# New constants in the duration model that sets the order of emission

## Chip, cores and metric

The kernel runs on one core of a Trainium2 chip. The metric is the device time of one execution in microseconds (us). Engines are called by name: TensorE (PE; PEld is its loading of weights), VectorE (DVE), ScalarE (ACT), GpSimd (POOL) and SyncE (SP), which issues nearly all transfers.

## What is computed

One step of a decoder trunk in float32, for one prompt of 256 tokens and 8 samples of 8 tokens, 320 tokens together. The width is 2048. Cut to its frame, the reference is:

```python
def trunk(x, c, states, p):
    for li in range(2):
        h, gate = modulate(x, c, ada_w, ada_b, norm_g)   # rmsnorm(x) * (1 + scale) + shift; silu(c) @ ada_w + ada_b
        if li == 0:
            z = h @ ab_w_in                              # q, k, v, r, g_lr, u
            o, s_gla = gla_mix(q, k, v, log_a, s0)       # gated linear attention, 4 heads
            y, h_re, h_im = s5_mix(u, ...)               # complex diagonal scan
            out = concat([o, y * sigmoid(y @ w_glu + b)]) @ ab_w_out
        else:
            z = h @ ml_w_in                              # q, k, v, og, gates
            hh, c1, n1, m1 = mlstm_mix(q, k, v, i_pre, logf, c0, n0, m0)   # 4 heads, a 512 x 256 state each
            out = (head_rmsnorm(hh) * sigmoid(og)) @ ml_w_out
        x = x + gate * out
        h, gate = modulate(x, c, ffn_ada_w, ffn_ada_b, ffn_norm_g)
        x = x + gate * ((silu(h @ w1) * (h @ w3)) @ w2)
    return rmsnorm(x), new states
```

## The kernel before

Activations stand feature-major, 128 features by 320 tokens. Every large product streams its weights through TensorE as 128 x 128 blocks. A float32 product is three passes of a shorter float format: weights and activations are split into a high and a low part, and each block gives three products of 320 columns (`hi` with `xh`, `lo` with `xh`, `hi` with `xl`). These are called stream products here; there are 18336. `load_to` loads a unit of 512 KB (24 stream products) from four buffers ahead, and `split_to` makes `hi` on ScalarE and `lo` on VectorE.

Everything else runs between the blocks as tasks, which are Python generators: the GLA and S5 mixers of layer 0, the mLSTM of layer 1, and the adaLN products (`Ada`: 192 steps, each with 1 MB of weights in one of two buffers and four products of 512 columns). After every three stream products `tick` looks at the tasks. It resumes one when the model says that what the task waits for is there (`due` asks `est.ready`), and when VectorE and ScalarE are not too far ahead of TensorE in the model.

The model is the class `Est`. Each instruction that is emitted is noted in it: `note` starts it when its engine and its operands are free, adds a duration from a formula, and keeps when the result can be read. A transfer gets an issue time, a time of the descriptor generator (`DGE`), bytes at a fixed rate on one server (`DMA`) and 1.0 us to land. No duration of the model is in the program that runs: it sets only which instruction is emitted before which. Where the program must wait for a task, `idle` and `wait` take adaLN steps or emit a product that nobody reads (`warm`), until the model's time has passed.

In the mLSTM (`ml_task`) each of 32 steps takes one sample's state, 512 KB, from one of three buffers `CR`: `load_c(g + 2)` at the end of step g, `store(g - 1)` at its beginning, both on SP's queue. `Ada.drip` takes one adaLN step every `gap` ticks at most, if `spare` finds its weights there in the model; `gap` is 2 in the first FFN.

## Time and profile before

| | us |
|---|---|
| median of 3 runs | 3397.55 |
| lowest and highest run | 3381.38 and 3400.94 |
| span of the profiled execution, first to last instruction | 3383.8 |
| TensorE busy in it | 3287.9 |
| VectorE busy in it | 1870.4 |
| ScalarE busy in it | 1327.8 |

For the profiled execution the span is the time that is known; it lies 13.8 us below the median of the runs and within their spread. Busy times of TensorE are modelled at their ends, so the starts of its instructions are the firmer number.

### The profile page before, as it was taken

The page shows a single profiled execution, that of the slowest core. Times are in us where ns is not written, and L with a number is a line of the kernel's source. Part 1 is how long each engine was busy: PE and PEld are TensorE (multiplying, and loading weights), DVE is VectorE, ACT ScalarE, POOL GpSimd, SP SyncE. Part 2 cuts the span into 40 slices and gives each one's busy share as a digit, 9 for nine tenths or more (in the row PEclk, how much of TensorE's full clock was granted, in tenths as well). Part 3 has the DMA queues.
Part 4 walks back from the last instruction along what each step waited for, and adds up shares of the span by engine and source line. Part 5 has one row for each costly group of instructions (what it writes and reads, how often), then busy time and mean ns, then how long its engine had stood idle before and what let it go on. Part 6 is the DMA issues. An engine that isn't in the chain of part 4 may idle for free.

```text
span 3383.8 us, 57931 instructions
## 1 busy us (share of the span) xinstructions
PE 3287.9 (97%) x22802; PEld 3023.7 (89%) x22802; DVE 1870.4 (55%) x3921; ACT 1327.8 (39%) x2509; POOL 336.9 (10%) x508
## 2 busy tenths in 40 slices
PE   7899889999999999999999999999999999999998
PEld 4687778887877799999998899999899999999997
DVE  3768767663344345445465665566645545545546
ACT  2354554343323333433434433344433343343343
POOL 0225511220000000000031000002200000000002
PEclk9999999999999999999999999999999999999999
DMA  9886678779999954444455665556564444444443
GB/s 305 291 264 219 194 259 305 269 240 322 317 318 320 320 171 149 150 152 148 151 170 145 191 194 144 177 187 206 184 207 149 152 150 150 150 150 150 150 150 100
DMA packets 597794, 686.66 MB, mean 203 GB/s; under 512 B 41097, under 2 KB 495057, under 8 KB 596945
## 3 DMA queue, kind: packets, MB, share of 16 engines
q1 hardware_dynamic: 594464, 680.26, 61.7%
q8 instruction: 179, 2.93, 0.3%
q10 hardware_dynamic: 3056, 2.70, 0.2%
q14 instruction: 95, 0.77, 0.1%
HBM read 643.19 MB, written 39.69 MB: 202 GB/s over the span
## 4 chain that ended last, share of the span: by engine, by line
PE 87%; DMA 5%; DVE 4%; ACT 2%; POOL 1%; issue 1%; SPq 0%; ACTq 0%; DVEq 0%; POOLq 0%
PE mm L220 74%; PE misc L220 8%; PE ada L220 5%; DVE S_slab L220 1%; POOL S_slab L220 1%; DVE lo L220 1%; DMA fix_slab<-in_ffn_ada_w_dram 1%; DVE X_slab L220 1%; DVE G_slab L220 1%; DMA R_slab<-in_state_mlstm_C_dram 1%; DMA fix_slab<-in_ab_w_in_dram 0%; DMA fix_slab<-in_ml_ada_w_dram 0%; DMA G_slab<-in_ab_ada_w_dram 0%; DMA fix_slab<-in_ab_ada_w_dram 0%; ACT hi L220 0%
## 5 line engine op out<-in xcount | busy, mean ns | idle before, releaser
L220 DVE TENSOR_TENSOR lo<-fix_slab,hi 128x512 fp32r<-128x512 f32 (+1 forms) x1556 | 1087.1, 704 | 1173.0 <-ACT hi L220 1168.9
L220 ACT CAST hi<-fix_slab 128x512 fp32r<-128x512 f32 (+1 forms) x1556 | 944.3, 612 | 1425.2 <-PE mm L220 1366.6
L220 PE MATMUL mm<-xh,hi 128*128 128x320 f32 x4704 | 1491.6, 317 | 9.7 <-DVE S_slab L220 5.9
L220 PE MATMUL mm<-xl,hi 128*128 128x320 f32 x4704 | 1460.7, 311 | 0.8 <-DVE xl L220 0.6
L220 PE MATMUL mm<-xh,lo 128*128 128x320 f32 x4704 | 1460.1, 310 | 0.9 <-DVE lo L220 0.9
L220 PEld LDWEIGHTS mm<-xh,hi 128*128 128x128 f32 x4704 | 888.4, 189 | 121.8 <-issue 88.0
L220 PEld LDWEIGHTS mm<-xh,lo 128*128 128x128 f32 x4704 | 889.2, 189 | 2.4 <-DVE lo L220 1.8
L220 PEld LDWEIGHTS mm<-xl,hi 128*128 128x128 f32 x4704 | 888.1, 189 | 2.2 <-DVE xl L220 2.2
L220 PE MATMUL mm<-ffh,hi 128*128 128x320 f32 x1408 | 437.8, 311 | 0.0
L220 PE MATMUL mm<-ffh,lo 128*128 128x320 f32 x1408 | 434.3, 308 | 0.0
L220 PE MATMUL mm<-ffl,hi 128*128 128x320 f32 x1408 | 434.3, 308 | 0.0
L220 POOL TENSOR_TENSOR X_slab<-X_slab 128x320 f32<-128x320 f32 (+1 forms) x117 | 109.9, 940 | 2062.4 <-DVE X_slab L220 2016.1
L220 PEld LDWEIGHTS mm<-ffh,hi 128*128 128x128 f32 x1408 | 264.4, 188 | 18.4 <-issue 17.6
L220 PEld LDWEIGHTS mm<-ffh,lo 128*128 128x128 f32 x1408 | 264.5, 188 | 0.0
L220 PEld LDWEIGHTS mm<-ffl,hi 128*128 128x128 f32 x1408 | 264.3, 188 | 0.0
L220 PE MATMUL ada<-fix_slab 128*32 128x512 f32 x1432 | 193.9, 616 | 12.7 <-DMA fix_slab<-in_ab_ada_w_dram 8.7
L220 POOL TENSOR_TENSOR S_slab<-S_slab 128x32 f32<-128x32 f32 (+3 forms) x226 | 119.5, 538 | 78.3 <-ACT S_slab L220 34.1
L220 DVE SCALAR_TENSOR_TENSOR ffs<-ffs,mm 128x320 f32<-128x320 f32 x176 | 81.4, 488 | 29.9 <-ACT ffs L220 23.8
L220 DVE SCALAR_TENSOR_TENSOR X_slab<-mm,fix_slab,X_slab 128x256 f32<-128x256 f32 x176 | 84.6, 480 | 16.7 <-PE mm L220 16.5
L220 PE MATMUL misc<-fix_slab 128*128 128x128 f32 (+1 forms) x454 | 73.1, 287 | 5.7 <-ACT fix_slab L220 5.6
L220 PEld LDWEIGHTS misc<-fix_slab 128*128 128x128 f32 x454 | 59.2, 171 | 18.2 <-ACT fix_slab L220 7.0
L220 PEld LDWEIGHTS ada<-fix_slab 128*32 128x32 f32 x1432 | 29.0, 108 | 51.0 <-issue 34.0
(151 smaller groups left out, 1812.9 us busy)
## 6 DMA issues: line engine op xcount, KB each, us to landing
fix_slab<-in_ffn_w_dram SPq DMA_DIRECT2D x524, 512.0 KB, 3.5
fix_slab<-in_ffn_ada_w_dram SPq DMA_DIRECT2D x96, 1024.0 KB, 7.6
fix_slab<-in_ml_ada_w_dram SPq DMA_DIRECT2D x48, 1024.0 KB, 7.2
fix_slab<-in_ml_w_in_dram SPq DMA_DIRECT2D x96, 512.0 KB, 4.4
fix_slab<-in_ab_ada_w_dram SPq DMA_DIRECT2D x35, 1024.0 KB, 8.0
fix_slab<-in_ab_w_in_dram SPq DMA_DIRECT2D x64, 512.0 KB, 6.5
R_slab<-in_state_mlstm_C_dram SPq DMA_DIRECT2D x32, 512.0 KB, 4.1
out_dram<-R_slab SPq DMA_DIRECT2D x32, 512.0 KB, 6.5
```

The source lines that it names most:

```text
L220: r = call(*a, **k)
```

## The change

Only the model's numbers are changed. Stream products get 0.0105 us more each, 0.1468 us instead of 0.1363. Plain float32 products get 0.04 us less where they are wide. A change between kinds of product (stream, products of 32 rows, others) costs TensorE 0.22 or 0.1 us more. The transfer server runs at 395 GB/s instead of 360, and SP's and ScalarE's transfers have a descriptor generator each. VectorE, ScalarE, GpSimd, the issue time and the landing time keep their formulas.

```diff
     def __init__(self):
-        self.t = dict.fromkeys(("PE", "DVE", "ACT", "POOL", "SP", "DGE", "DMA"), 0.0)
+        self.t = dict.fromkeys(("PE", "DVE", "ACT", "POOL", "SP", "DGESP", "DGEACT", "DMA"), 0.0)
         self.wr, self.rd, self.alias = {}, {}, {}
         self.end = 0.0
+        self.kind = None
...
                 self.t[eng] = t + 0.06
-                t = self.t["DGE"] = max(self.t["DGE"], t) + 0.45
-            t = self.t["DMA"] = max(self.t["DMA"], t + 0.65) + 4e-3 * int(np.prod(out.shape)) / 360
+                t = self.t["DGE" + eng] = max(self.t["DGE" + eng], t) + 0.45
+            t = self.t["DMA"] = max(self.t["DMA"], t + 0.65) + 4e-3 * int(np.prod(out.shape)) / 395
             fin = t + 1.0
...
                 elif ins[0].dtype == F32R:
-                    d = n / 2400 + 0.003
+                    d = n / 2400 + 0.0135
                 else:
-                    d = max(1.67e-3 * n + 0.05, 0.2 + 5e-4 * n)
+                    d = max(1.67e-3 * n + 0.01, 0.22)
+
+                kind = "stream" if ins[0].dtype == F32R and n == T else "tiles" if ins[0].shape[1] == 32 else "other"
+                if kind != self.kind:
+                    d += 0.22 if self.kind is None or "stream" in (kind, self.kind) else 0.1
+                self.kind = kind
```

The instructions are the same on every engine, but for 8 `warm` products (327 products of their form before, 319 now) and two elementwise operations that VectorE now does in place of GpSimd. On TensorE the kinds of product change 900 times in the old order and 877 times in the new. What moves is where the tasks stand in the stream.

First place: TensorE in `ml_task`, from the state update (`km`, `vs`) of the fifth step of the first head. `mm` rows are stream products, and the `misc` rows from `fix_slab` are the first of the next step. Before:

```order
L220 MATMUL misc1_17083<-km_16132,vs_16131 128x256 x2
L220 MATMUL misc2_17087<-km_16132,vs_16131 128x256 x2
L220 MATMUL mm_16954<-xh_95,hi0_83 128x320
L220 MATMUL mm_16954<-xh_95,lo0_89 128x320
L220 MATMUL mm_16954<-xl_96,hi0_83 128x320
L220 MATMUL mm_16955<-xh_95,hi0_83 128x320
L220 MATMUL mm_16955<-xh_95,lo0_89 128x320
L220 MATMUL mm_16955<-xl_96,hi0_83 128x320
```

Now:

```order
L226 MATMUL misc0_16987<-km_16104,vs_16103 128x256 x2
L226 MATMUL misc1_16991<-km_16104,vs_16103 128x256 x2
L226 MATMUL mm_16640<-xh_95,hi1_84 128x320
L226 MATMUL mm_16640<-xh_95,lo1_90 128x320
L226 MATMUL mm_16640<-xl_96,hi1_84 128x320
L226 MATMUL misc2_16999<-fix_slab_80 128x128
L226 MATMUL misc0_17003<-fix_slab_80,R_slab_16099 128x128 x4
L226 MATMUL misc1_17009<-fix_slab_80,R_slab_16099 128x128 x4
```

Between this update and the next step stood 24 stream products, of which six are shown (3, 6, 15, 24, 24, 27 and 24 after the eight steps of the head); now there are 3 after every update, and 9 more within each step. From update to update the first head has 12, 15, 24, 33, 33, 36 and 33 stream products before and 12 each time now, and the other heads the same. On SP's queue a weight load stood in nearly every step; now there is one in every second.

Second place: TensorE in the first FFN, where an `ada` row is one adaLN step. Before, at the closest pair that there is:

```order
L220 MATMUL mm_7764<-xh_95,lo0_89 128x320
L220 MATMUL mm_7764<-xl_96,hi0_83 128x320
L220 MATMUL mm_7765<-xh_95,hi0_83 128x320
L220 MATMUL mm_7765<-xh_95,lo0_89 128x320
L220 MATMUL mm_7765<-xl_96,hi0_83 128x320
L220 MATMUL mm_7764<-xh_95,hi1_84 128x320
L220 MATMUL mm_7764<-xh_95,lo1_90 128x320
L220 MATMUL mm_7764<-xl_96,hi1_84 128x320
L220 MATMUL mm_7765<-xh_95,hi1_84 128x320
L220 MATMUL mm_7765<-xh_95,lo1_90 128x320
L220 MATMUL mm_7765<-xl_96,hi1_84 128x320
L220 MATMUL ada_7747<-fix_slab_80 32x512 x4
```

Now, at a pair of the same weights:

```order
L226 MATMUL ada_7634<-fix_slab_80 32x512 x4
L226 MATMUL mm_7647<-xh_95,hi0_83 128x320
L226 MATMUL mm_7647<-xh_95,lo0_89 128x320
L226 MATMUL mm_7647<-xl_96,hi0_83 128x320
L226 MATMUL mm_7646<-xh_95,hi0_83 128x320
L226 MATMUL mm_7646<-xh_95,lo0_89 128x320
L226 MATMUL mm_7646<-xl_96,hi0_83 128x320
L226 MATMUL ada_7634<-fix_slab_80 32x512 x4
```

The closest two steps stood 12 stream products apart and now stand 6 apart. Over this stretch the same 94 adaLN steps stood between the 2613th and the 5034th stream product and now stand between the 2604th and the 4329th.

The third place is layer 0, where the mixers' products stood between the 645th and the 2109th stream product and now stand between the 606th and the 1545th. The second pass of S5 took 375 stream products (1092 to 1467) and takes 237 (933 to 1170); the last three heads of GLA took 290 to 390 each and take 130 to 150.

## Rows read from the trace of the kernel before

**Rows 1.** The page: span, and each engine's busy time, share and instructions.

```profile
span 3383.8 us, 57931 instructions
...
PE 3287.9 (97%) x22802; PEld 3023.7 (89%) x22802; DVE 1870.4 (55%) x3921; ACT 1327.8 (39%) x2509; POOL 336.9 (10%) x508
```

**Rows 2.** Table of stretches: length, busy us (instructions) of each engine, PEclk, DMA share, GB/s.

```profile
25.00:50.00 25.00, 17.11 (x110) 8.05 (x110) 10.40 (x34) 4.53 (x11) 1.58 (x6) 0.86 1.06 396
50.00:75.00 25.00, 24.31 (x159) 18.32 (x159) 8.91 (x16) 10.70 (x23) 0.00 (x0) 0.93 0.99 343
200.00:500.00 300.00, 270.82 (x1982) 228.49 (x1981) 217.94 (x576) 149.12 (x370) 126.03 (x245) 0.97 0.71 229
1200.00:1760.00 560.00, 560.00 (x3824) 560.00 (x3823) 290.99 (x523) 215.67 (x370) 26.80 (x28) 1.00 0.49 152
1870.00:2290.00 420.00, 413.85 (x3181) 385.75 (x3180) 256.49 (x531) 168.83 (x331) 28.11 (x31) 1.00 0.59 181
```

**Rows 3.** Waits of SP, 1870 to 2290 us: us in total, times, longest.

```profile
SPq L220 <- DMA out_dram<-R_slab: 144.4, 27, 6.9
```

**Rows 4.** Issues on SP's queue in order of time: start, us, tensors.

```profile
1877.39 0.38 SPq L220 DMA_DIRECT2D out_dram<-R_slab  x1
1882.37 0.37 SPq L220 DMA_DIRECT2D R_slab<-in_state_mlstm_C_dram  x1
...
1883.34 0.50 SPq L220 DMA_DIRECT2D out_dram<-R_slab  x1
1890.75 0.37 SPq L220 DMA_DIRECT2D R_slab<-in_state_mlstm_C_dram  x1
...
1898.08 0.37 SPq L220 DMA_DIRECT2D R_slab<-in_state_mlstm_C_dram  x1
```

**Rows 5.** The page, transfers of the matrix states: count, size, us to landing.

```profile
R_slab<-in_state_mlstm_C_dram SPq DMA_DIRECT2D x32, 512.0 KB, 4.1
out_dram<-R_slab SPq DMA_DIRECT2D x32, 512.0 KB, 6.5
```

**Rows 6.** TensorE in order of time, first products of four state steps: start, us.

```profile
1876.43 0.27 PE L220 MATMUL misc<-fix_slab 128*128 128x128 f32 x1
...
1881.35 0.27 PE L220 MATMUL misc<-fix_slab 128*128 128x128 f32 x1
...
1887.16 0.27 PE L220 MATMUL misc<-fix_slab 128*128 128x128 f32 x1
...
1917.12 0.27 PE L220 MATMUL misc<-fix_slab 128*128 128x128 f32 x1
```

**Rows 7.** Waits of TensorE, 1870 to 2290 us.

```profile
PE misc L220 <- DMA R_slab<-in_state_mlstm_C_dram: 2.9, 4, 1.1
```

**Rows 8.** TensorE in order of time around one adaLN step.

```profile
903.97 0.31 PE L220 MATMUL mm<-xl,hi 128*128 128x320 f32 x1
904.21 1.06 PE L220 MATMUL ada<-fix_slab 128*32 128x512 f32 x8
905.20 0.41 PE L220 MATMUL mm<-xh,hi 128*128 128x320 f32 x1
```

**Rows 9.** Transfers from 2530 to 2900 us: share of 16 engines, then issues.

```profile
q1 hardware_dynamic: 55713, 55.34, 47.8%
...
fix_slab<-in_ffn_w_dram SPq DMA_DIRECT2D x105, 512.0 KB, 3.5
```

**Rows 10.** Transfers from 900 to 1200 us.

```profile
q1 hardware_dynamic: 64341, 94.45, 90.7%
...
fix_slab<-in_ffn_ada_w_dram SPq DMA_DIRECT2D x33, 1024.0 KB, 7.0
fix_slab<-in_ffn_w_dram SPq DMA_DIRECT2D x63, 512.0 KB, 4.9
fix_slab<-in_ml_ada_w_dram SPq DMA_DIRECT2D x25, 1024.0 KB, 7.4
```

**Rows 11.** Waits of TensorE, 200 to 500 us.

```profile
PE misc L220 <- ACT S_slab L220: 9.8, 4, 7.3
```

## The prediction

> **What bounds the kernel now.** I read the page first, then the table of stretches, then the waits and the issue times of the stretches that looked different. The page says that TensorE is busy for 3287.9 of 3383.8 us [rows 1]. So the change can only gain from some 96 us of idle time, while everything that it makes TensorE wait for is lost. In the table of stretches, look at 1200 to 1760 us: 3824 products in 560.0 us without a gap, 0.1465 us each [rows 2]. That is the price of a stream product wherever nothing is in its way. Between 200 and 500 us, where the two mixers of layer 0 run, it is busy only 270.8 of 300 us. Between 1870 and 2290 us, where the mLSTM runs, 413.8 of 420 us: nearly full, and the question is what keeps it so.
>
> The change leaves every instruction of computation in place. It is a change of interleaving, and it must be costed by asking at each place how much stream work still covers a wait.
>
> **The matrix states of the mLSTM.** Each of 32 steps (4 heads, 8 samples) loads a state of 512 KB, updates it and stores it. Three buffers serve, so the load for step g + 2 goes into the buffer of step g - 1 and stands on SP's queue right behind that store. The trace shows that SP really waits there for the store to land: 144.4 us in 27 waits [rows 3], and on SP's queue the store at 1877.39 holds the next load until 1882.37, the one at 1883.34 until 1890.75 [rows 4]. From load to load it is 7.33 us (1890.75 to 1898.08) with a weight load between them; without one I put 0.5 us of issue and the 4.98 us of the first store, 5.5 us, an estimate. A state lands a median 4.1 us after its issue [rows 5].
>
> What does TensorE put against this? From 1881.35 to 1887.16 is one step with 24 stream products [rows 6]: 5.81 - 24 x 0.1465 = 2.29 us of its own work. From 1876.43 to 1917.12 are six steps with 174 products in the order: 6 x 2.29 + 174 x 0.1465 = 39.2 us of work in 40.7 us. So the 33 products a step of the old order just cover the chain, and 1.5 us a head is lost. TensorE waits for these states only 2.9 us in all four heads [rows 7].
>
> The new order has 12 products in every step, so a step is 2.29 + 1.76 = 4.05 us of work, and six are 24.3 us. The chain does not shrink as much. Counted from the second step, the first store is issued after 0.96 us, the load behind it at 5.94, and it lands at 10.0 us, which starts the fourth step; four more periods follow to the eighth. The new order puts a weight load into every second step, so the period is the mean of 5.5 and 7.33, 6.4 us: the eighth step starts at 10.0 + 25.7 = 35.7 us. That is 11.4 us of waiting a head, 9.9 more than now, **40 us** for four heads. With 5.5 us a period it is 25 us, with 7.33 us 54 us. The products that left these steps come later, where nothing waits for them, so the cover is not paid back. The model puts a store's landing 0.06 + 0.45 + 0.65 + 1.33 + 1.0 = 3.5 us after its issue; the trace has 6.5 [rows 5]. That is why it sees no wait.
>
> **The adaLN weights during the first FFN.** 94 adaLN steps (1 MB of weights each) ran between the 2613th and the 5034th stream product, and now run between the 2604th and the 4329th: 1725 products instead of 2421. An adaLN step takes TensorE 905.20 - 903.97 - 0.147 = 1.08 us [rows 8]. The work of that stretch is 1725 x 0.1465 + 94 x 1.08 = 354 us. Now the DMA engines: a weight load of the stream costs 0.478 x 370 / 105 = 1.68 us of all sixteen engines [rows 9], and 24 products use one. From 900 to 1200 us, 58 adaLN loads and 63 weight loads took 0.907 x 300 = 272 us [rows 10], so an adaLN load is (272 - 63 x 1.68) / 58 = 2.87 us. The new stretch asks for 94 x 2.87 + 1725 / 24 x 1.68 = 391 us at a share of 1.00. The mixed stretch at 50 to 75 us reached 0.99, the one at 25 to 50 us, with adaLN loads alone in flight, 1.06 [rows 2]. I take 1.00, as the stretch is mixed: 391 - 354 = 37 us, less some 7 us for the two loads already landed and the weight buffers filled, **30 us** of waiting for adaLN weights where the trace now has almost none. At 1.06 it is 369 - 354 - 7 = 8 us. At the 0.907 that is reached now it is 431 - 354 - 7 = 70 us, but that share was set by what was asked for.
>
> The Trainium skill has a rule here, in "DMA: Bandwidth & Descriptors", section "Specifications": about 358 GB/s from HBM for one core. The stretch moves 94 x 1.049 + 72 x 0.524 = 136 MB, 381 us by that rate, a wait of 27 us before the 7; the trace does not agree with it as a limit, as it has 396 GB/s from 25 to 50 us [rows 2], by which there would be no wait.
>
> **The mixers of layer 0.** Their products stood between the 645th and the 2109th stream product and now end at the 1545th: some 525 fewer products, 77 us less cover over a chain through VectorE, ScalarE, GpSimd and small DMAs. What such a chain costs when it is late shows in the waits from 200 to 500 us: TensorE waits 9.8 us in 4 waits for ScalarE's copies into S_slab, the longest 7.3 us [rows 11]. The lower bound is a gain of 29 us, all idle time of that stretch [rows 2]; the upper is 77 us, if all the cover was needed. The second pass of the S5 scan has 8 stages of the same make, so I let each have one such wait of the mean 2.45 us: 19.6 instead of 9.8, **10 us** more. The durations in the model for VectorE and ScalarE are untouched, so nothing in it warns of these waits better than before.
>
> **What it saves.** Eight fewer products of the kind that nobody reads, priced at the 0.27 us of the 128-column products in [rows 6], and 877 instead of 900 changes between kinds of product. A change costs 904.21 - 903.97 - 0.147 = 0.09 us [rows 8]. Together **4 us**. Start and end I put at nothing: the first 100 us are bound by transfers of the same bytes, and the last norm by the chain after the last product. If the cover at the start is worse, a load is late there by some microseconds.
>
> **Sum.** 40 + 30 + 10 - 4 = 76 us on the profiled span of 3383.8 us, so 3460 us. The median of the runs shown, 3397.55 us, lies 13.8 us above that span, and the span is near the fastest run; I add the sum to the median: **3474 us**.
>
> **Rivals.** *Faster.* The model of TensorE is now true, and tasks are resumed when their data is there: the 29 us of idle time from 200 to 500 us go, and the 6 us from 1870 to 2290 [rows 2], with the 4 us saved: 3397.6 - 39 = 3359 us. It decides by one number: a store must land within 4.05 - 0.46 = 3.6 us, so that a step of 12 products covers the chain. Against it, the shortest store in the rows held SP for 4.98 us [rows 4], and the adaLN stretch would need a share of 1.10.
>
> *Nothing to measure.* The waits exist but at their lower bounds: 25 us at the states, 8 us at the adaLN weights, a gain of 10 us in the mixers and the 4 us, 19 us in all: 3417 us. Or the order is undone by waits that sit elsewhere anyway. For it speaks that TensorE is 97% busy in either order and that all bytes are the same.
>
> *The clock.* In the long waits of the states TensorE is busy 4.05 of 6.4 us, 63%. From 25 to 50 us it was busy 17.11 of 25 us and the granted clock was 0.86; from 1870 to 2290 us it was busy 98% and the clock 1.00 [rows 2]. At 0.86 a step's work is 4.7 us and still fits. If the clock stays at its lower level, 1.2 GHz, in the five late steps of each head, the work is 8.1 us and replaces the period of 6.4: 20 x 1.7 = 34 us more, 3508 us. The Trainium skill tells of this in "TensorE: Matmul & The Clock Gate", section "HAM oscillation — how this bites in real kernels": waits for data between groups of products bring the slow clock back each time. The row of 25 to 50 us agrees in kind, not in full.
>
> *The mixers need all their cover:* 77 us there instead of 10: 3541 us.
>
> **How the numbers follow.** Forecast 0.55, with its own range of 3430 to 3515 from the bounds of its terms; nothing to measure 0.17; faster 0.08; the clock 0.12; the mixers 0.08. A measurement of this kernel can tell about 1% from no change, 34 us. Slower by more than that: 0.55 + 0.12 + 0.08 = 0.75; within it 0.17; faster 0.08. For 8 in 10 the range goes from 3395 to 3530 us: it leaves out the faster case, the lowest part of the one without a difference, and the mixers in full.
>
> **What the new profile would show.** For the states: TensorE's waits for loads of the mLSTM state rise from 2.9 us to about 45 us, in five steps of each head with 6 to 7 us from load to load on SP. For the adaLN weights: a DMA share near 1.00 in the first FFN, TensorE's waits for adaLN weights near 30 us, and then a stretch of pure stream. For the mixers: idle time of TensorE for S_slab and G_slab near 40 us instead of 29. Wrong would be a store that lands in under 4 us once fewer weights stand before it, a DMA share above 1.05 over 350 us, or a mixing stretch whose idle time goes.

## The result, and the profile after

The changed kernel takes 3531.57 us (median of 4 runs, 3529.99 to 3533.24) against 3390.43 us (3381.38 to 3400.94): a ratio of 1.0418, 95% interval 1.0392 to 1.0445. It is slower, as forecast, by 141 us, where the forecast was 76.

The page of the changed kernel, span and TensorE's busy time, the lines that answer to [rows 1]:

```profile
span 3530.2 us, 57923 instructions
...
PE 3343.3 (95%) x22786; PEld 3060.0 (87%) x22786; DVE 1875.9 (53%) x3921; ACT 1330.4 (38%) x2509; POOL 326.7 (9%) x506
```

The span grew by 146.4 us, TensorE's busy time by 55.4 us with 16 records fewer, its idle time by 91 us. So there are two things to find: waits, and products that take longer. The table of stretches (columns as in [rows 2]) shows where:

```profile
200.00:500.00 300.00, 260.77 (x1746) 211.05 (x1746) 201.74 (x544) 128.92 (x325) 123.86 (x248) 0.89 0.67 219
760.00:1185.00 425.00, 383.13 (x2564) 282.63 (x2563) 145.76 (x289) 114.65 (x201) 3.85 (x5) 0.98 0.89 318
1865.00:2430.00 565.00, 523.63 (x3760) 481.42 (x3761) 318.04 (x669) 212.51 (x418) 38.73 (x48) 0.97 0.54 159
```

In the mixers (first line) both show: 39 of 300 us idle, and a granted clock of 0.89 where [rows 2] have 0.97. In the first FFN (second line) TensorE is idle for 42 of 425 us while the DMA share is 0.89, not 1.00. In the mLSTM it is idle for 41 of 565 us.

The stream has 18336 products in the same order in both kernels, so both traces can be cut at the same products, by the start times of a product with a given number. "Waits" are the gaps over 0.4 us from a product's end to the next one's start; a side product is any that is neither stream nor adaLN.

| stream products | before | after | difference | waits | stream products | side products |
|---|---|---|---|---|---|---|
| 645 to 2545, mixers of layer 0 | 508.1 | 552.5 | +44.3 | 31.6, now 50.6 | 297.8, now 307.5 | 127.9, now 141.3 |
| 2545 to 5034, first FFN | 488.5 | 538.7 | +50.1 | 0.9, now 37.3 | 385.8, now 396.0 | 8.2, now 10.4 |
| 8882 to 11995, mLSTM | 633.1 | 675.6 | +42.5 | 11.2, now 40.2 | 476.0, now 482.8 | 144.1, now 151.6 |
| 11995 to 12459, adaLN of the second FFN | 93.3 | 100.1 | +6.7 | | | |

Everything else together is +3 us. A record of a stream product lasts 0.31 us, and the next starts 0.147 us later [rows 8]; so of each wait some 0.16 us stand in the product columns and not under waits, about 5 us of the first FFN's, which has 31 waits. Now what TensorE waits for (waits of TensorE: total, times, longest), first 150 to 690 us, which holds the mixers, then 740 to 1290 us in the first FFN, then the mLSTM, 1960 to 2560 us:

```profile
PE ada L226 <- DMA fix_slab<-in_ffn_ada_w_dram: 21.3, 14, 2.5
PE misc L226 <- DVE S_slab L226: 9.2, 6, 2.8
PE misc L226 <- ACT S_slab L226: 7.1, 5, 2.9
PE misc L226 <- DVE G_slab L226: 4.3, 4, 2.1
...
PE ada L226 <- DMA fix_slab<-in_ab_ada_w_dram: 3.3, 3, 2.9
```

```profile
PE ada L226 <- DMA fix_slab<-in_ffn_ada_w_dram: 21.6, 22, 4.3
PE ada L226 <- DMA fix_slab<-in_ml_ada_w_dram: 19.7, 22, 2.2
```

```profile
PE misc L226 <- DMA R_slab<-in_state_mlstm_C_dram: 23.9, 16, 2.3
```

In 150 to 690 us the kernel before waited for adaLN weights like this:

```profile
PE ada L220 <- DMA fix_slab<-in_ab_ada_w_dram: 4.0, 3, 2.2
...
PE ada L220 <- DMA fix_slab<-in_ffn_ada_w_dram: 1.9, 3, 1.2
```

The changed kernel's waits for the state loads answer to [rows 7], and the next line to [rows 3]: SP still waits in the mLSTM for the stores to land, and a store and a load there take 5.2 and 4.7 us, where [rows 5] have 6.5 and 4.1.

```profile
SPq L226 <- DMA out_dram<-R_slab: 92.5, 24, 5.7
```

```profile
out_dram<-R_slab SPq DMA_DIRECT2D x32, 512.0 KB, 5.2
R_slab<-in_state_mlstm_C_dram SPq DMA_DIRECT2D x30, 512.0 KB, 4.7
```

From one state load to the next SP takes 6.7 and 5.7 us here; the second pair has a weight load between (2001.29), the first has none.

```profile
1992.62 0.37 SPq L226 DMA_DIRECT2D R_slab<-in_state_mlstm_C_dram  x1
...
1999.32 0.37 SPq L226 DMA_DIRECT2D R_slab<-in_state_mlstm_C_dram  x1
...
2001.29 0.37 SPq L226 DMA_DIRECT2D fix_slab<-in_ml_w_in_dram  x1
2005.00 0.37 SPq L226 DMA_DIRECT2D R_slab<-in_state_mlstm_C_dram  x1
```

Over the four heads, the first period of each left out, 22 such periods are 5.3 to 6.9 us long, 5.9 us on average: 5.8 with a weight load between and 6.1 without.

So at two of the three expected places TensorE waits for what was expected, the state loads and the adaLN weights. The wait for adaLN weights in the mixers was not expected at all.

### The profile page after: what moved, and what is told of

The parts are those of the page before. It is cut to its first block, busy times and chain, and to the rows that moved or that the text cites. A ratio compares the mean times of both kernels' runs of the same rounds, so it can differ in the third digit from the quotient of the medians.

```text
span 3530.2 us, 57923 instructions
## 1 busy us (share of the span) xinstructions
PE 3343.3 (95%) x22786; PEld 3060.0 (87%) x22786; DVE 1875.9 (53%) x3921; ACT 1330.4 (38%) x2509; POOL 326.7 (9%) x506
## 5 line engine op out<-in xcount | busy, mean ns | idle before, releaser
L226 PEld LDWEIGHTS ada<-fix_slab 128*32 128x32 f32 x1432 | 29.5, 109 | 117.0 <-DMA fix_slab<-in_ffn_ada_w_dram 47.6
L226 POOL TENSOR_TENSOR S_slab<-S_slab 128x32 f32<-128x32 f32 (+3 forms) x226 | 111.3, 502 | 81.3 <-ACT S_slab L226 32.8
L226 PE MATMUL misc<-fix_slab,R_slab 128*128 128x128 f32 (+4 forms) x314 | 47.3, 287 | 34.6 <-DMA R_slab<-in_state_mlstm_C_dram 23.9
L226 ACT COPY fix_slab<-ada 128x512 f32<-128x512 f32 x48 | 28.1, 586 | 134.2 <-PE ada L226 134.1
```

Of the source, the lines that this page charges most:

```text
L226: r = call(*a, **k)
```

## The experiments

Eighteen kernels were timed, all made from the changed one by the edits shown. The last three columns are differences from the kernel before, in us, over the stretches of the table above.

| kernel | median us | ratio to before, 95% interval | mixers | first FFN | mLSTM |
|---|---|---|---|---|---|
| changed | 3531.57 | 1.0418 (1.0392 to 1.0445) | +44.3 | +50.1 | +42.5 |
| e1_store_landing | 3498.51 | 1.0318 (1.0291 to 1.0345) | +47.3 | +52.2 | +1.8 |
| e2_load_landing | 3498.35 | 1.0310 (1.0284 to 1.0337) | +54.6 | +24.9 | +30.9 |
| e3_both_landings | 3450.46 | 1.0174 (1.0147 to 1.0202) | +35.5 | +23.0 | +1.1 |
| e4_transfers_as_before | 3507.26 | 1.0340 (1.0310 to 1.0369) | +43.2 | +40.0 | +40.9 |
| e5_even18 | 3620.78 | 1.0661 (1.0643 to 1.0680) | +47.0 | +149.0 | +36.4 |
| e6_even18_three | 3509.57 | 1.0337 (1.0311 to 1.0363) | +44.3 | +31.6 | +41.9 |
| e7_even24 | 3573.89 | 1.0534 (1.0504 to 1.0564) | +50.4 | +103.0 | +40.8 |
| e8_fill_mixers | 3534.33 | 1.0409 (1.0384 to 1.0435) | +48.8 | +53.8 | +34.5 |
| e9_no_interruptions | 3449.20 | 1.0165 (1.0144 to 1.0186) | +29.2 | +14.2 | +18.3 |
| e10_no_interruptions_landings | 3413.36 | 1.0056 (1.0038 to 1.0075) | +13.4 | +8.5 | -0.7 |
| e11_even18_asked_early | 3548.93 | 1.0461 (1.0445 to 1.0477) | +47.6 | +60.0 | +46.1 |
| e12_even18_early_three | 3495.78 | 1.0303 (1.0285 to 1.0320) | +54.8 | +6.1 | +45.0 |
| e13_small_stores | 3516.90 | 1.0359 (1.0332 to 1.0386) | +50.5 | +51.4 | +17.9 |
| e14_mixers_fewer_adaln | 3554.75 | 1.0464 (1.0429 to 1.0499) | +65.3 | +54.8 | +40.6 |
| e15_three_places | 3464.63 | 1.0203 (1.0175 to 1.0230) | +53.8 | +6.6 | +12.0 |
| e16_other_engines | 3509.59 | 1.0366 (1.0341 to 1.0391) | +62.8 | +15.6 | +35.9 |
| e17_all_measured | 3417.56 | 1.0092 (1.0072 to 1.0113) | +33.6 | +14.6 | -3.9 |
| e18_all_measured_three_buffers | 3408.93 | 1.0069 (1.0052 to 1.0087) | +30.9 | -2.1 | -6.2 |

A stretch whose order is the same comes out within 11 us from one profiled execution to another in the mixers (the changed kernel, e5 to e7 and e11 to e13: +44.3 to +54.8), within 5 us in the first FFN (the changed kernel, e1, e8, e13 and e14: +50.1 to +54.8) and within 8 us in the mLSTM (the changed kernel, e5 to e8 and e14: +34.5 to +42.5). A smaller difference in these columns shows nothing.

### The landing of transfers in the model

```diff
-            fin = t + 1.0
+            fin = t + (3.5 if out.space == bass.MemoryType.DRAM else 1.0)   # e1
+            fin = t + (1.0 if out.space == bass.MemoryType.DRAM else 2.5)   # e2
+            fin = t + (3.5 if out.space == bass.MemoryType.DRAM else 2.5)   # e3
```

> The changed kernel with one number more in the model: a transfer to DRAM is done 3.5 us after its bytes instead of 1.0 (the state's store then lands in the model about 6 us after its issue; the trace has 6.5). In the order the state products of the mLSTM heads stand 24 to 30 stream products apart again, not 12; the 93 adaLN steps of the first FFN stay where the change put them. Theory (the store that SP holds the next state load behind bounds the heads): products 8882 to 11995 lose the 42 us that they gained, and the kernel takes 3480 to 3495 us. Rival (the late state steps cost by the clock or by their lack of cover, whatever the store does): the heads keep 25 us or more of the 42, 3515 to 3530 us.

> The changed kernel with one number more in the model: a transfer to SBUF is done 2.5 us after its bytes instead of 1.0 (a weight load of 1 MB then lands about 6.2 us after its issue in the model; the trace has 7 or more). 20 of the adaLN steps of the first FFN stand in its last 705 products again (27 before the change, 1 behind it), and 38 instead of 45 in the first 900 products of the mixers. Theory (two buffers of adaLN weights are asked for faster than they land): most of the 37 us of waits in products 2545 to 4329 goes, so 3490 to 3505 us with the heads as slow as now. Rival (the 50 us of the first FFN are interruptions of the stream and a lower clock, not waits): less than 12 us are won, 3520 us or more.

> Both numbers of the two kernels above together. If the three stages add up, the gains of the two add to within 10 us: 3440 to 3465 us; what is left over the kernel before is then the mixers of layer 0, which keep 25 to 45 us. Rival (one stage's loss comes back in another when it is taken away here): the sum of the two gains is missed by over 15 us.

e1 came out as its theory said in the mLSTM, which is back to within 1.8 us of before, with the rest as slow as in the changed kernel; its time, 3498.51 us, is 3.5 us above the range. One number in a model, which only spaces the state steps, gives back 41 of 42.5 us. In its trace TensorE's waits for the state loads are no longer among its waits, although SP waits longer for the stores (waits of SP, 1960 to 2560 us):

```profile
SPq L226 <- DMA out_dram<-R_slab: 126.4, 24, 7.0
```

That is the point about engines off the path: waits of SP of 126 us together cost next to nothing when there is stream work over them, while with waits of 92 us the stretch is 42 us longer.

e2 gives back 25 us in the first FFN, where 20 adaLN steps stand late again, and takes its waits from 37.3 to 16.3 us. It is in its range with some luck: the heads were to stay as slow as they were and gave back 12 us, and the mixers took 10 more. e3 gains 81 us, 15 more than e1 and e2 together (33 each), where within 10 was expected; the surplus lies in the mixers, which the two numbers together spread somewhat (502 of the mixers' products stand in stream products 645 to 1545; 554 and 560 with one of the numbers alone).

### Which part of the change moves the work

e4 puts the transfers back, e9 the interruptions and the float32 products, and e10 adds both landings to e9.

```diff
+            t = self.t["DMA"] = max(self.t["DMA"], t + 0.65) + 4e-3 * int(np.prod(out.shape)) / 360   # e4, with one DGE
...
-                    d = max(1.67e-3 * n + 0.01, 0.22)
+                    d = max(1.67e-3 * n + 0.05, 0.2 + 5e-4 * n)                                       # e9, e10
-                if kind != self.kind:
+                if False:                                                                             # e9, e10
```

> The changed kernel with the transfers in the model as before (360 instead of 395, one DGE instead of one for each of SP and ACT); the durations of products and the interruptions stay as changed. In the order the state products of the heads stand 12 apart as in the changed kernel, and 13 instead of 1 adaLN steps lie in the last 705 products of the first FFN. Theory (the products' longer durations alone make the transfers look shorter in the model's time): the heads stay at +42, the first FFN gives back 12 to 25 of its 50 us, 3500 to 3520 us. Rival (the transfers' numbers did it): 3430 us or less.

> The changed kernel with the model's interruptions and its mixer products as before (no 0.22 or 0.10 us where TensorE goes from the stream to something else; the float32 product's old two terms); transfers and the stream product's 0.0135 stay changed. In the order 34 adaLN steps and 489 mixer products stand in stream products 645 to 1545 (changed kernel 45 and 560, before 26 and 442), 31, 44 and 19 steps in the first FFN, and the state products of the heads 9 to 24 apart. Theory (each term added to a TensorE duration packs the side work closer in stream products; mixers and states cost by how close): all three stages give back about half, 3455 to 3485 us. Rival (the mixers' 43 us come from the transfers or the stream product's term): the mixers keep 35 us or more, 3495 us or more.

> The kernel before this one with both landing times of the third experiment (3.5 us for a store, 2.5 for a load). The order stands near that of before in every stage: 24 adaLN steps and 457 mixer products in products 645 to 1545, 29, 43 and 23 steps in the first FFN, state products up to 39 apart. Theory (the time is set by that packing alone): within 25 us of the kernel before, 3395 to 3420 us; of the 30 us that the mixers kept in the third experiment 8 or fewer are left. Rival (something else in the changed numbers costs): 3430 us or more.

The transfers' numbers are a small part (24 us, 10 of them in the first FFN, a little under what was expected). The interruptions and side products are the largest: without them 82 of 141 us are back, more than the half that I expected: 36 of 50 us in the first FFN and 24 of 42 in the mLSTM, but only 15 of 44 in the mixers. e10 stands at 1.0056, in its range, though its mixers keep 13.4 us where 8 or fewer were expected. By the code of the model, each us that the model adds to TensorE lets fewer stream products pass in the time that it gives to a transfer or to another engine, and those durations were not raised with it.

### What bounds the first FFN

The share of the DMA engines stayed at 0.89, so either they can't do more in this mixture, or too few loads are asked for. These five kernels tell that apart. All but e7 have the changed kernel's rate, 93 adaLN steps in products 2545 to 4329 (94 in the changed kernel), but evenly 18 or 21 products apart (e7: 24 or 27).

```diff
-                    if self.s >= self.last or not self.spare():
+                    if self.s >= self.last or not (self.step() if self.gap == 6 else self.spare()):   # e5, e6; e7 with 8
-                    ada.gap, ada.last = 2, 176
+                    ada.gap, ada.last = 6, 176                                                        # e5, e6; e7 with 8
...
+                    ada.x3 = p.tile([P, 4, 512], F32, name="ada3")[:, :, :]                           # e6, e12
+                    ada.free.append(ada.x3)                                                           # e6, e12
...
+                    elif self.s >= self.last or clock[0] < at:                                        # e11, e12
+                        self.load()   # every second tick, as spare() does, not only in the next step
+                        self.post()
+                    else:
+                        self.step()
+                        at = clock[0] + 6
```

> The changed kernel, but in the first FFN an adaLN step every 18 or 21 stream products whatever the model says of its weights: as many steps per product as in the changed kernel (38, 54 and 2 in products 2545 to 3300, 3300 to 4329 and behind; the change has 38, 55 and 1), but never two of them 6 to 12 products apart; still two weight buffers. Theory (the rate of the transfers bounds: 94 loads of 1 MB beside the stream's own weights in about 400 us): the waits of 37 us stay within 10, and the kernel takes 3520 to 3540 us. Rival (the uneven spacing does it: the second step of a close pair can't have landed): at least 20 of the 37 us go, 3490 to 3512 us.

> The same order as the kernel before it, with a third 1 MB buffer for adaLN weights in the first FFN, so that each load is asked for one step earlier. Theory of the rate (DMA engines are full): no more than 6 us less than with two buffers. Rival (two buffers and the landing of 7 us bound, the engines have room): the waits that two buffers leave go, the DMA share of that stretch rises above 0.93, and the kernel takes 12 us or more off the two buffers' time.

> As the first of these, with a step every 24 or 27 stream products (29, 41 and 24 steps; before the change 26, 40 and 27), two buffers. Both theories of the first FFN: its 50 us go but for 5, since neither rate nor close pairs are left: 3480 to 3492 us. If more than 15 us of the 50 stay, what costs is the adaLN steps that stand in the mixers and not those in the FFN.

> The kernel with a step every 18 to 21 products and two buffers again, but each freed buffer's load is asked for at the next tick of 6 products, as the changed kernel asks, and not at the next step (the earlier one asked for it a step later, and so had one load under way where the changed kernel has up to two). Theory of the landing (a load takes 5.5 to 7 us from its issue, and a step comes every 4 us): waits of products 2545 to 4329 go from 102 us to 40 or less, 3515 to 3545 us, no better than the changed kernel's 37 since its rate is the same. Rival (uneven spacing costs in the changed kernel): waits under 17 us, under 3512 us.

> The same with the third buffer, loads asked for early: three of them can be under way. Theory of the landing: waits under 8 us and the stretch of products 2545 to 4329 some 12 to 20 us below the three buffers asked late (410 us), 3485 to 3500 us. Rival (with two loads under way the transfers' rate is the bound, so a third gives nothing): within 5 us of the three buffers asked late, 3504 to 3516 us, with the DMA share of that stretch at 0.95 or more.

e5 and e7 missed both of their theories, by 80 us and more, and the reason is in the edit: `spare()` asks for the next load each time it looks, `step()` only when the next step is there. So a load was asked for one step before its use, no longer nearly two. e11 repairs that; its waits, 48.0 us, and its time are still above what was expected (40 us or less, 3545 us at most). e6 and e12 came out as the landing has it. Stretches of e5, e11, the changed kernel, e6 and e12, 800 to 1100 us:

```profile
800.00:1100.00 300.00, 242.36 (x1489) 182.32 (x1488) 79.21 (x142) 67.64 (x119) 0.00 (x0) 0.91 0.73 262
```

```profile
800.00:1100.00 300.00, 268.55 (x1798) 199.47 (x1797) 96.96 (x184) 79.94 (x140) 0.00 (x0) 0.98 0.89 316
```

```profile
800.00:1100.00 300.00, 271.92 (x1847) 200.27 (x1845) 99.30 (x193) 81.02 (x141) 0.00 (x0) 1.00 0.91 325
```

```profile
800.00:1100.00 300.00, 285.10 (x1935) 211.23 (x1935) 104.85 (x207) 85.13 (x147) 0.00 (x0) 0.99 0.95 339
```

```profile
800.00:1100.00 300.00, 299.92 (x2060) 223.08 (x2054) 111.23 (x217) 89.83 (x155) 0.00 (x0) 1.00 0.99 360
```

The lead in this table is what TensorE has to do, in the program, between the request for a load and the step that uses it: stream products at 0.1465 us [rows 2] and steps at 1.08 us [rows 8].

| kernel | lead, worked out | products 2545 to 4329, us | waits there, us |
|---|---|---|---|
| e5, two buffers | 18 products, 1 step: 3.7 us | 526.8 | 102.0 |
| e7, two buffers, a step every 24 or 27 | 24 products, 1 step: 4.6 us | 433.1 (70 steps) | 55.8 |
| e11, two buffers | 30 products, 1 step: 5.5 us | 443.3 | 48.0 |
| changed, two buffers, uneven | some 32 products, 1 step: 5.8 us | 434.7 | 37.3 |
| e6, three buffers | 36 products, 2 steps: 7.4 us | 410.5 | 22.7 |
| before, two buffers, a step every 27 | some 47 products, 1 step: 8.0 us | 349.0 (66 steps) | 0.9 |
| e12, three buffers | 48 products, 2 steps: 9.2 us | 389.7 | 5.6 |

TensorE goes from 242 busy us in 300 to 299.92, at the same number of steps and bytes per stream product; the waits for adaLN weights of e12 in 740 to 1290 us are a single line, where the changed kernel has 41.3 us:

```profile
PE ada L226 <- DMA fix_slab<-in_ffn_ada_w_dram: 2.7, 2, 2.2
```

A load of 1 MB takes 7.0 and 7.4 us to land in [rows 10], and in the changed kernel, 800 to 1100 us:

```profile
fix_slab<-in_ml_ada_w_dram SPq DMA_DIRECT2D x48, 1024.0 KB, 6.6
...
fix_slab<-in_ffn_ada_w_dram SPq DMA_DIRECT2D x19, 1024.0 KB, 6.3
```

So the engines had room, and the bound is the landing of a load against the lead with which it is asked for: under 6 us of lead there are 37 us of waits and more, at 7.4 us 22.7, and from 8.0 us on 0.9 and 5.6. Uneven spacing is not what costs: e11 is even and no better. The Trainium skill's "DMA: Bandwidth & Descriptors", section "Specifications", gives about 358 GB/s from HBM for a core; e12 moves 360 GB/s here with a share of 0.99, near that figure; as a limit the trace doesn't agree with it, since 25 to 50 us have 396 GB/s [rows 2]. The Trainium skill's "Trainium Kernel Development and Optimization", section "Best Practices", advises to double-buffer so that transfers overlap with computing; at the new rate of steps two buffers, asked early, left 37.3 and 48.0 us of waits in this stretch and three 5.6, while at the rate of before two were enough (0.9 us).

### The state store

```diff
-                    sp.dma_start(out=o[11][0, g % 8, g // 8].rearrange("(y p) d -> p y d", p=P), in_=CR[g % 3].v(4, 256))
+                    sp.dma_start(out=o[11][0, g % 8, g // 8].rearrange("(y p) d -> p y d", p=P)[0:8],
+                                 in_=CR[g % 3].v(4, 256)[0:8])
```

> The changed kernel, same order, but the store of a state writes 8 of its 128 partitions (32 KB, not 512 KB), so that most of the new states are left out of the output. Theory (SP holds the next state load until the store has landed, and that period of 6 to 7 us is what 12 products a step don't cover): with a store that lands in 2 to 3 us the heads lose 30 us or more of their 42, 3485 to 3502 us. Rival (the load's own landing of 4 us, or the chain from a landed state through ScalarE and VectorE, is the long part): the heads keep 20 us or more, 3510 to 3530 us.

It fell between the two: the mLSTM gave back 24.6 us, where the theory had 30 or more and the rival 22 or less; the time, 3516.90 us, is in the rival's range. What the theory speaks of did go. TensorE's waits for state loads fell from 23.9 to 1.1 us, SP's for stores from 92.5 to 40.2 (1960 to 2560 us, TensorE and then SP):

```profile
PE misc L226 <- DMA R_slab<-in_state_mlstm_C_dram: 1.1, 3, 0.6
```

```profile
SPq L226 <- DMA out_dram<-R_slab: 40.2, 19, 4.1
```

The 17.9 us that stayed are not waits over 0.4 us (14.0 us, 11.2 before) but products that take longer: 6 us more for the same 3113 stream products and 10 us more for the same 1392 records of side products. Spacing takes that back as well (e1: 3 us and nothing). The store's bytes went with its hold on SP, and no run takes the two apart.

A part of the longer products is the clock. The stretch of products 8882 to 11995, before and in the changed kernel:

```profile
1768.35:2401.45 633.10, 620.96 (x4522) 585.96 (x4522) 383.15 (x796) 255.62 (x499) 69.25 (x78) 0.99 0.56 173
```

```profile
1865.31:2540.87 675.56, 634.19 (x4515) 592.06 (x4514) 384.96 (x796) 256.59 (x499) 66.04 (x76) 0.97 0.54 162
```

The granted clock was 0.98 in e13 and 0.99 in e1. The clock's records in the traces have it at its lower level, 0.5 of full speed, for 17 us of this stretch before, 34 in the changed kernel, 27 in e13 and 17 in e1. A microsecond at half speed costs at most half of one, so the clock can be at most 9 of the changed kernel's 14 us of longer products, and 5 of e13's 16; what the rest is was not shown.

### The mixers of layer 0

e8 fills waits, e14 moves adaLN steps out of the mixers, e15 mends each of the three places by itself, e16 to e18 also raise the other engines' durations.

```diff
+        def noted(*a, **k):                       # e8: for TensorE, FILL_AT = {910: 8, 954: 15, ... 2520: 8}, 26 places
+                if self.n in FILL_AT:
+                    self.fill(FILL_AT[self.n])    # so many products of ones and ident, not noted in the model
...
-            ada.gap = 3
+            ada.gap = 8                           # e14, e15
-        ada.gap, ada.last = 3, 80
+        ada.gap, ada.last = 8, 80                 # e14, e15
...
-                d = 0.095 + 0.83e-3 * n           # ScalarE
+                d = 0.185 + 0.85e-3 * n           # e16, e17, e18
-                d = 0.065 + (6.26e-3 if op == "reciprocal" else 1.04e-3) * n
+                d = 0.155 + (6.26e-3 if op == "reciprocal" else 1.04e-3) * n
...
-                d = 0.095 + n * (0.83e-3 if op == "memset" else 4e-3 if op == "tensor_scalar" else 2.27e-3)   # GpSimd
+                d = 0.095 + n * 0.83e-3 if op == "memset" else 0.3 + n * (3.1e-3 if op == "tensor_scalar" else 2e-3)
```

e15 has e1's line and e12's buffer too; e17 is e16 with e3's line, e18 is e17 with e12's buffer.

> The changed kernel, same order, with 156 products of 128x128 that nobody reads put ahead of the 26 products that waited over 0.5 us in stream products 645 to 1545 (44.5 us of waits; each fill is somewhat shorter than its wait). Theory (the mixers' 43 us are half waits, half a clock that falls to 1.2 GHz in and behind them): with TensorE at work through the waits the clock stays up, stream and mixer products of that stretch take some 15 to 25 us less, 3506 to 3518 us. Rival (waits alone; the slower products are not the clock's doing or the clock falls anyway): within 5 us of the changed kernel or slower by what the fill overshoots, 3527 to 3545 us.

The stretch from 200 to 580 us of the changed kernel, then of e8:

```profile
200.00:580.00 380.00, 332.08 (x2237) 264.45 (x2237) 247.64 (x683) 158.68 (x395) 136.56 (x271) 0.90 0.71 235
```

```profile
200.00:580.00 380.00, 340.96 (x2516) 278.21 (x2514) 243.96 (x670) 153.37 (x381) 132.41 (x268) 0.97 0.70 230
```

The clock did stay up, 0.97 against 0.90, but the time did not fall, so by its numbers the rival holds. It doesn't settle the matter, for a reason that stands in TensorE's waits of e8 (L408 is the fill):

```profile
PE misc L408 <- ACT S_slab L233: 10.0, 2, 5.1
PE ada L233 <- DMA fix_slab<-in_ffn_ada_w_dram: 8.7, 8, 1.9
PE misc L408 <- DVE G_slab L233: 5.4, 4, 1.9
PE misc L408 <- DVE S_slab L233: 4.8, 2, 2.7
```

For 20.2 us the fill itself waited (it reads constants, so it is its bank in PSUM that wasn't free), and then ran after the wait and not in it. Over products 645 to 2545 the waits fell by 11.3 us, while 310 records of fill came in, 43.2 us from each start to the next, a part of which is the end of the product ahead of the fill (at the 0.09 us of 96 records of this form in e12's first FFN, 8.6 us, they would be 28). Stream products went from 307.5 to 296.6 us (303.3 to 309.4 in all executions of this order without the fill) and adaLN steps from 53.0 to 51.1; the stretch is 4.4 us longer, which is within its spread. So with the slower clock of the changed kernel's mixers these products were 13 us longer, and the other side products by an amount that the fill hides; that this would also come off the time was not shown.

> The changed kernel with an adaLN step at most every 8 ticks in the mixers, not every 3: 27 steps in stream products 645 to 1545 and 21 in 1545 to 2322 (45 and 3 in the changed kernel, 26 and 21 before); 527 of the mixers' products still stand in the first of the two (560 and 442). Theory A (the mixers lose by waits for adaLN weights, 24.6 us there against 3.7 before): products 645 to 2545 give back 18 to 30 of their 43 us, 3500 to 3514 us. Theory B (they lose because the chain of mixer work through the other engines has too few stream products under it): waits for adaLN weights go and waits for S_slab and G_slab rise, 8 us or less come back, 3523 to 3533 us.

Neither. Waits for these weights fell, but the stretch got 21 us longer: the mixers' own waits rose, as B says, by more than what was won (waits of TensorE, 150 to 690 us).

```profile
PE misc L226 <- DVE G_slab L226: 18.2, 11, 7.5
PE ada L226 <- DMA fix_slab<-in_ffn_ada_w_dram: 13.4, 8, 5.4
PE misc L226 <- ACT S_slab L226: 10.5, 5, 2.8
```

That an adaLN step between two mixer products is itself work that lies over the mixers' chain would explain it; no run shows this by itself.

> The changed durations of products and transfers are kept; each place is mended by itself: adaLN steps every 8 ticks in the mixers, a store's landing of 3.5 us in the model, three adaLN buffers with a step every 18 products in the first FFN. If the three causes are separate and cover the loss, the parts add up: about 33 us at the heads and 36 to 44 in the first FFN, with 5 to 30 from the mixers: 3425 to 3460 us. If they overlap, 3470 us or more.

The mLSTM gave back 30 us and the first FFN 44, near what was expected, and the mixers, where 5 to 30 us were to be won, stand at +53.8, within the spread of the changed kernel's order; so it misses its range by 5 us. The first two causes are separate; the mixers' mending was none, as in e14.

> The changed kernel with the durations of the other engines in the model raised to what the trace of before has in the mixers (VectorE 0.48 us for 128x256 and 0.32 for 128x128, so 0.155 + 1.04 n / 1000 instead of 0.065; ScalarE 0.47 for 128x320, so 0.185 + 0.85 n / 1000 instead of 0.095; GpSimd 0.35 for 32 columns and 0.83 for 256). In the order only 365 of the mixers' products stand in stream products 645 to 1545 (560 in the changed kernel, 442 before), and 25 adaLN steps (45, 26); state steps stay 12 apart, the first FFN 30, 51 and 1. Theory (the mixers' chain through the other engines needs stream products under it, and the model's durations for those engines were too short): products 645 to 2545 come within 10 us of before, 3480 to 3500 us. Rival (the mixers' loss comes from something that the order of their products doesn't govern): they stay 25 us or more above, 3510 us or more.

> The kernel before this one with both landing times of the third experiment as well, so that every engine and the transfers have durations near the measured ones. Order: 20 adaLN steps and 319 mixer products in products 645 to 1545; 26, 44 and 22 steps in the first FFN; state steps 30 apart. If the loss was an incomplete model (TensorE's times true, everything that it waits for too short), the kernel is back at before, 3385 to 3410 us; if true durations by themselves make a worse order, 3425 us or more.

> The same with three adaLN buffers and a step every 18 products in the first FFN (34, 56 and 2 steps). In the experiment with three buffers that stretch came within 6 us of before; so no more than 8 us from the kernel before this one, 3380 to 3410 us. It beats the kernel before the change only if the mixers win more than 10 us by their wider spacing.

My theory of e16 fell: by its numbers the rival holds, but not by its reason. The mixers were spread more widely than before the change (365 of the mixers' products in stream products 645 to 1545, 442 before), and cost 62.8 us more than before, not 10 or less. Products 645 to 1545 did become 10.9 us shorter than before, but 1545 to 2322 became 71.2 us longer: 126 products of the form of `warm` stand there in the order (35 before, 4 in the changed kernel), 94 of them `warm` itself by the trace's records (15 before, none in the changed kernel); together they take 36.0 us, 5.6 before. The stream needs the mixers' result at product 2322, and what comes too late is waited for with `warm` products. e17 lies between its two cases: the mLSTM is as fast as before (-3.9 us, within the spread), the mixers are 33.6 us slower. e18 is in its range, and as fast as before in both other stretches (-2.1 and -6.2 us, within their spread), but it doesn't win in the mixers. No kernel here beats the one before the change.

## Why the prediction was wrong

The sign and the three places were right; the sum, 76 us against 146 on the span, was too small, and 3531.57 lies above the range, just. The two terms that were mis-sized are the 30 us of the adaLN weights (50.1) and the 10 us of the mixers (44.3).

**The states of the mLSTM: right in size by some luck, half right in kind.** Forecast 40, measured 42.5. e1 shows that their close order is the cause, and e13 that the store, by its hold on SP or by its bytes, is 25 us of it. But TensorE's waits for state loads rose from 2.9 only to 23.9 us, not to about 45, and all its waits there by 29. The period of 6.4 us was too long: I let a weight load on SP's queue lengthen it from 5.5 to 7.33 us, but measured it is 5.9 us, and a weight load between makes no difference (5.8 with, 6.1 without). With 5.9 us my own sum gives 31 us, not 40. Longer products in the close order, 14 us, which the forecast didn't have, made up for it. The clock can be at most 9 us of them; the rest is not explained.

**The adaLN weights in the first FFN: the step that failed is "I take 1.00, as the stretch is mixed".** Forecast 30, measured 50.1. The share stayed at 0.89 to 0.91. I had the end for 0.907 in hand, 70 us, and put it aside with "but that share was set by what was asked for". So it was, but by two buffers and the moment of the request, and these didn't change with the order; the lead went from 8.0 to 5.8 us, below the 6.3 to 7.4 us of a landing. e12 reached the share of 0.99 that I took, and its stretch takes 389.7 us, where I had 391 for the engines. But it has hardly a wait: TensorE's work in it is 384 us, where my prices give 362 for its 1784 products and 93 steps (my 354 was for 1725 and 94). The stream products around the steps take 0.158 us each and not 0.1465, and 92 side products, which I left out, take 8.2 us. So at a share of 1.00 my 30 us would have been wrong as well, to the other side.

**The mixers of layer 0: the step that failed is the 10 us for "eight stages", each with one wait of 2.45 us.** Measured 44.3, and up to 54.8 in other executions of this order. Two things were not in it. The 19 us of new waits are waits for adaLN weights, 24.6 us in the changed kernel and 5.9 before: I looked for that wait only in the first FFN, but the same change moved 19 more adaLN steps into products 645 to 1545 (26 before, 45 after). And 25 us are longer products (stream 9.7, side 13.4, adaLN 2.1), while the granted clock went from 0.97 to 0.89 in 200 to 500 us. e8 ties 13 us or more of those 25 to the clock: by the traces' clock records the lower level held for 78 us of this stretch (17 before, 27 in e8), and the stream products in it took 0.29 us each. So the rival of the clock was right about a price, and wrong about the main place: it foresaw the state steps, where the clock is 0.97. The rival of the mixers that need all their cover gave 77 us there, 33 us too much, as my 10 is 34 too little; that its 3541 us is the nearest to the measured time of all is luck, as it has the other terms as I had them. e9 and e10 fit it in kind: with 489 and 457 of the mixers' products in stream products 645 to 1545 they cost 29.2 and 13.4 us, with 560 it is 44.3. But their spread is 11 us, and e14 and e16 say that cover is not the whole. What stays open is which chain sets the end of the mixers: in the changed kernel, where work stands close, it waits and the clock falls; in e16, where it stands wide, it misses its product in the stream. The order before the change is the best of all that were run.

**Savings of 4 us, and start and end at nothing.** They can't be seen beside the rest. Missing from the sum were 6.7 us in the second FFN, for adaLN weights again, and 3.1 us at the norm before the mLSTM.

**Rivals.** *Faster* decided by a store that lands in under 3.6 us; the median in the mLSTM is 5.2 us. *Nothing to measure* would have needed each wait at its lower bound; none was.

**Why a truer model of TensorE was worse.** The change raised TensorE's durations towards the measured ones and left what TensorE waits for too short: a store that lands in 3.5 us in the model and in 6.5 in [rows 5], loads, the other engines' operations. That errors on both sides partly cancelled before is my reading; two kernels fit it. e10 removes the added time and mends the landings: 1.0056. e17 keeps it and mends the rest: 1.0092. That order, not any of the numbers as such, is the cause is shown for the mLSTM by e1, where nothing but the order changed, and for the first FFN by e11 and e12, where the time of the request and a third buffer set the waits; for the mixers it is open.

## What to carry to other kernels

A planner's durations must be true relative to one another: when one engine's times are set to what was measured, set those of the transfers' landing and of the other engines in the same step, and read what the trace says of each. For a stream of loads, first set the landing time against the lead from request to use, and then the bytes against the rate of the engines; here a DMA share of 0.9 with a consumer that waits asked for another buffer or an earlier request, not for fewer bytes. When a change packs side work more closely, look in every stretch into which it is packed, and not only where it is taken from.

## What the runs showed of the hardware that I had not expected

- Loads of 1 MB asked for 3.7, 5.5 and 9.2 us ahead, beside the weight stream, gave DMA shares of 0.73, 0.89 and 0.99, and 262, 316 and 360 GB/s; asking 1.8 us later made the stretch of 93 loads 84 us longer, 54 us of it waits (e5 against e11), with a granted clock of 0.91 and 0.98 in 800 to 1100 us.
- A store of 32 KB still holds SP's next load for 2.1 us on average (40.2 us in 19 waits); one of 512 KB for 3.9 us in the changed kernel (92.5 in 24) and 5.3 us before (144.4 in 27, [rows 3]).
- With 26 waits over 0.5 us in 386 us, 44.5 us together (products 645 to 1545), the granted clock of 200 to 580 us was 0.90, where it was 0.98 before the change; with products of no use in part of the waits it was 0.97 (e8). The stretch of the kernel before:

```profile
200.00:580.00 380.00, 348.35 (x2524) 292.45 (x2522) 279.06 (x757) 188.49 (x459) 134.96 (x260) 0.98 0.74 243
```
